# Four token groups instead of three in the input product of a hybrid decoder layer

## The chip, the cores and the metric

The kernel runs on one core of one Trainium2 chip, written in Bass with a tile framework that orders the instructions of each engine by priorities and sets the semaphores. The metric is the device time of one execution in microseconds. The profiler's record of one execution stands beside it, with start and duration of each instruction on TensorE (PE, with its weight loads as PEld), VectorE (DVE), ScalarE (ACT), GpSimd (POOL) and the DMA queues of SyncE (SP) and ACT.

## The reference

One layer of a decoder trunk on 1040 tokens (16 meta tokens ahead of 1024), width 1024, all float32. `h` is the layer-normed input. Cut to what matters:

```python
z = h @ w_in + b_in                       # 1024 -> 3840 columns
q, k, v, c_in, gates = split(z, [512, 640, 768, 1792])
a = swa_sink_attention(q, k, v, ...)      # window 128, 8 heads, 2 kv heads, sinks, T5 bias
y_attn = a @ w_attn_proj
c = c_val * sigmoid(c_gate)               # halves of c_in, 512 each
c = silu(layer_norm(causal_dwconv(c, 31 taps)))
y_conv = c @ w_conv_proj
mixed = sigmoid(g_attn) * y_attn + sigmoid(g_conv) * y_conv
h = layer_norm(alpha * h + mixed @ w_out)
u, g = split(causal_dwconv(h @ ffn_w_up, 3 taps), 2)
out = layer_norm(alpha * h + (gelu(g) * u) @ ffn_w_down)   # meta tokens dropped
```

## The kernel before

The layout is columns of `z` on the 128 partitions and tokens along the free dimension. A float32 product is made of float32r halves: weights and activations are each split into hi and lo, and every 128-row term of a product is three matmuls, hi·hi (L296), hi·lo (L300) and lo·hi (L301), in `product`. The sum over the 8 terms of K = 1024 is thus 24 matmuls into one PSUM tile, and each matmul loads its 128 × 128 weights anew.

`z` has 30 tiles of 128 columns. Three of them (k, v and the first q tile) belong to the lead-in (0 to 55 us), which also norms and transposes the input; its products are written out by hand in three token groups `HG` of 272, 384 and 384. The other 27 go through `z_tile`: for each token group, `z_group` takes a PSUM tile `ps_z` (three buffers), calls `product`, and hands the result to an evacuation. Their order is: convolution chunk 1 and 0 (two tiles each, gate and value), q tiles 1 to 3, gate tile 0, then gate tiles 1 to 15 and convolution chunks 2 and 3. Convolution tiles use the groups `HG`; q and gate tiles use `TG`, the same groups with the first 14 tokens (`U0`) left out, so 258, 384 and 384 columns.

The activations are in two arenas of 8320 columns, `RHO` (terms 0 to 3) and `RHC` (terms 4 to 7). `h0(k, hl, a, b)` gives the place of term k, half hl, tokens a to b. Before the change, each group has a region of its own: group 0 in slots of 272, groups 1 and 2 in slots of 384 from columns 272 and 3344 on (one slot of group 0 stays at 0, the others lie from 6144 on).

The evacuations: `q_evac` scales on ACT into a staging buffer (`stage`, in the arena `FA`), splits into `qsh` (ACT) and `qsl` (DVE), two buffers each, and stores both to `qd` in DRAM, the hi half on ACT's queue and the lo half on SP's. `gate_evac` (ACT, L672) takes a tanh into a staging buffer and stores it to `sgd` on ACT's queue. Convolution tiles stage the sigmoid of one tile (ACT) and multiply it into the other (DVE, L656); 31 taps of each chunk then run on DVE (L665), 1280 ns for each of the 120 later taps.

Attention is by blocks of 128 queries: `load_q` reads the queries back from `qd` into `qt`, the band scores are matmuls at L829 and L830, and the two queries ahead of the first block have small score matmuls (L749, L750). Priorities set the order: the band of attention stands ahead of the z tiles, so its matmuls are woven between those of the gate tiles. One edge is written by hand: the L749 matmuls are put behind a product term of gate tile 0, called `ahead`; `chunks_done` lists the first matmul of each product term, and before the change it takes the entry 2·8 + 1 after the tile's first. The edge orders instructions, and no semaphore is waited on for it.

After the z tiles come the branch projection (`ps_p`, L296 to L301 through the same `product`, with the groups `PG` of 258, 256, 256 and 256 tokens and the operand slots of `place`), the out product (`ps_w`), and the feed-forward's up (L1499) and down (L1637) products.

Of the kernel before, what the change touches and what calls it, by code (L numbers as in the profile page):

```python
# [31 lines left out]
KC = D // P  # L32
# [3 lines left out]
U0 = 14  # L36
# [14 lines left out]


HG = [(0, 272), (272, 656), (656, 1040)]
UG = [(0, 258), (258, 642), (642, 1026)]

PG = [(0, 258), (258, 514), (514, 770), (770, 1026)]
# [43 lines left out]
def tile_hybrid_layer(  # L100
# [9 lines left out]
    def load(o, i):  # L110
        return nc.sync.dma_start(out=o, in_=i)
# [5 lines left out]
    def f32(ap):  # L117
        return ap.bitcast(F)
# [6 lines left out]
    @contextmanager  # L125
    def rank(p):

        saved = tc.cur_priority
        tc.cur_priority = p
        yield  # L130
        tc.cur_priority = saved
# [9 lines left out]
    FA = arena.tile([P, 6144], F, name="FA")  # L141
    RHC = arena.tile([P, 8320], R, name="RHC")
    RHO = arena.tile([P, 8320], R, name="RHO")
# [62 lines left out]
    def bcol(m):  # L206
        return colA[:, m:m + 1]
# [43 lines left out]


    def h0(k, hl, a, b):
        g = next(g for g, x in enumerate(HG) if a < x[1])
        x, y = HG[g]
        i, n = (k % 4) * 2 + hl, y - x
        o = i * n + ((6144 if i else 0), 272, 3344)[g]
        return (RHO if k < 4 else RHC)[:, o + a - x:o + b - x]


    tc.cur_priority = RK_QKV
# [13 lines left out]
    def weights(shape, fill):  # L275
        fills[0] += 1
        n = fills[0]
        own = n == 3
        raw = sp.tile(shape, F, name="wr3") if own else wraw(shape)
        with rank({1: 13, 2: 18, 3: 17, 4: 23}.get(n, RK_SPLIT)):  # L280
            last_fill.append(fill(raw))
        hi, lo = (sp.tile(shape, R, name=t + "3") if own else wsp_p.tile(shape, R, name=t, tag=t)
                  for t in ("whi", "wlo"))
        if n <= 3:
            return hi, lo, raw
        with rank(RK_SPLIT):
            last_split.append(split(raw, hi, lo, True))
        return hi, lo

    chunks_done = []  # L290
# [13 lines left out]
    def z_group(wt, g, a, b, evac):  # L304
        hi, lo = wt
        ps = pat.tile([P, 512], F, name="ps_z", tag="mm", bufs=3)
        product(ps[:, :b - a], [(hi[:, k], lo[:, k], h0(k, 0, a, b), h0(k, 1, a, b)) for k in range(KC)])
        with rank(RK_EVAC):
            evac(g, a, b, ps[:, :b - a])

    def z_tile(fill, groups, evac, wt=None):
        wt = wt or weights([P, KC, P], fill)
        for g, (a, b) in enumerate(groups):
            z_group(wt, g, a, b, evac)

    def in_cols(m):
        return lambda raw: load(raw, w_z[m])

    TG = [(a + U0 if i == 0 else a, b) for i, (a, b) in enumerate(HG)]

    st_next = [0]

    def stage(n, lo=4104, cnt=5):
        i = st_next[0] % cnt
        st_next[0] += 1
        return FA[:, lo + i * 400:lo + i * 400 + n]

    tc.cur_priority = RK_QKV + 1000

# [15 lines left out]
    def q_evac(r):  # L345
        def evac(g, a, b, ps):
            t = stage(b - a)
            nc.scalar.activation(t, ps, AF.Identity, bias=qb[:, r:r + 1], scale=HD ** -0.5)
            h, l = (qsp.tile([P, 400], R, name=n, tag=n)[:, :b - a] for n in ("qsh", "qsl"))
            nc.scalar.copy(h, t)  # L350
            nc.vector.tensor_tensor(l, t, f32(h), OP.subtract)
            for hl, (put, x) in enumerate(((store, f32(h)), (load, f32(l)))):
                c = 0
                if g == 0:
                    c = P + 2
                    put(qd[:, (hl * 4 + r) * c:(hl * 4 + r + 1) * c], x[:, :c])
                n = (b - a - c) // P
                if n == 0:
                    continue
                i = (a - U0 + c) // P  # L360
                put(dram(qd, q_at(i) + (hl * 4 + r) * P, [[8 * U, P], [8 * P, n], [1, P]]),
                    x[:, c:].rearrange("p (n q) -> p n q", q=P))
        return evac
# [87 lines left out]
    def turns(g, *ks):  # L451
        n = len(GT[g])
        c = HG[g][1] - HG[g][0]
        at = {}
# [9 lines left out]
    def scaled(g, *ks):  # L464
        a, b = HG[g]
        for k in ks:
            tm = FA[:, 1044 + 272 * k:][:, :272] if g == 0 else sp.tile([P, 384], F, name="tm", tag="tm", bufs=5)
            ac(nc.scalar.activation(tm, turned[g, k], AF.Identity, bias=b0col(k), scale=g0col(k)))
            tms[g, k] = tm

    def parts(g, *ks, hi_act=()):
        a, b = HG[g]
        for k in ks:
            tm = tms[g, k]
            if k in hi_act:
                ac(nc.scalar.copy(h0(k, 0, a, b), tm))
            else:
                dv(V.tensor_copy(h0(k, 0, a, b), tm))
            dv(V.tensor_tensor(h0(k, 1, a, b), tm, f32(h0(k, 0, a, b)), OP.subtract))
# [131 lines left out]
    wt_c1 = [weights([P, KC, P], in_cols(m)) for m in (11, 7)]  # L611
# [30 lines left out]
    def conv_chunk(c):  # L642
        sig = {}

        def g_evac(g, a, b, ps):
            sig[g] = stage(b - a)

            nc.scalar.activation(sig[g], ps, AF.Tanh, bias=bcol(10 + c), scale=0.5)
            nc.scalar.activation(sig[g], sig[g], AF.Identity, bias=half_, scale=0.5)

        z_tile(in_cols(10 + c), HG, g_evac, wt_c1[0] if c == 1 else None)
        cin = cp.tile([P, 16 + T], F, name="cin", tag="cin")
        nc.vector.memset(cin[:, 0:16], 0.0)

        def v_evac2(g, a, b, ps):
            nc.vector.scalar_tensor_tensor(cin[:, 16 + a:16 + b], ps, bcol(6 + c), sig[g], OP.add, OP.mult)  # L656

        z_tile(in_cols(6 + c), HG, v_evac2, wt_c1[1] if c == 1 else None)
        with rank(RK_CONV + c * 100):
            for j in range(TAPS):  # L660
                wc = cdw[:, j * CH + c:j * CH + c + 1]
                if j == 0:
                    nc.vector.tensor_scalar(acc[c], cin[:, j:j + U], wc, cdwb(c), OP.mult, OP.add)
                else:
                    nc.vector.scalar_tensor_tensor(acc[c], cin[:, j:j + U], wc, acc[c], OP.mult, OP.add)  # L665

    def gate_tile(i):
        b2, m = divmod(i, KC)

        def gate_evac(g, a, b, ps):  # L670
            t = stage(b - a)
            nc.scalar.activation(t, ps, AF.Tanh, bias=bcol(14 + i), scale=0.5)  # L672
            store(sgd[b2, m, :, a - U0:b - U0], t)

        z_tile(in_cols(14 + i), TG, gate_evac)

# [31 lines left out]
    for q4 in range(2):  # L708
        ps = pat.tile([P, 512], F, name="ps_v4", tag="t", bufs=2)
        for i in range(4):  # L710
            c = NMETA + (q4 * 4 + i) * P
            nc.tensor.transpose(ps[:, i * P:(i + 1) * P], vT[:, c:c + P], ident)
        src = ps[:, :].rearrange("p (n g d) -> p n g d", g=2, d=HD)
        for g in range(NKV):
            hi, lo = (V[:, q4 * 4:q4 * 4 + 4, g, i] for i in range(2))
# [6 lines left out]
    for r in range(1, 4):  # L722
        z_tile(in_cols(r), TG, q_evac(r))

# [11 lines left out]
    tc.cur_priority = RK_Z - 500  # L736
    first_chunk = len(chunks_done)
    gate_tile(0)
    ahead = chunks_done[first_chunk + 2 * KC + 1]

    tc.cur_priority = RK_ATT

# [3 lines left out]
    for h in range(NH):  # L746
        g, r = divmod(h, 4)
        o = ps[:2, h * 16:(h + 1) * 16]
# [144 lines left out]
    with rank(RK_EVAC):  # L893
        nc.scalar.copy(c_hi[:, :U], csum)
        pinned.append(nc.vector.tensor_tensor(c_lo, csum, f32(c_hi[:, :U]), OP.subtract))
        for g, (a, b) in enumerate(UG):
            means[g] = pat.tile([P, 512], F, name="ps_m", tag="st"[g % 2], bufs=2)
# [40 lines left out]
    def cln_centre(g):  # L938
        a, b = UG[g]
        for c in range(CH):  # L940
            pin(dve.tensor_tensor(acc[c][:, a:b], acc[c][:, a:b], means[g][:, :b - a], OP.subtract))

    def cln_var(g):
        a, b = UG[g]
        n = b - a
        s_ = temp(n)
        nc.scalar.activation(s_, acc[0][:, a:b], AF.Square)
        for c in range(1, CH):
            q_ = temp(n)
            nc.scalar.activation(q_, acc[c][:, a:b], AF.Square)  # L950
            pin(dve.tensor_tensor(s_, s_, q_, OP.add))

        hi, lo = (conv(1, hl, a, b) for hl in range(2))
        pin(dve.tensor_copy(hi, s_))
        pin(dve.tensor_tensor(lo, s_, f32(hi), OP.subtract))
        sums[g] = pat.tile([P, 512], F, name="ps_m", tag="s", bufs=2)
        mean_mms(sums[g][:, :n], ones_r, hi, lo)

    def cln_rstd(g):
        n = UG[g][1] - UG[g][0]  # L960
        pv_, r_, t_ = sums[g][:, :n], temp(n), temp(n)
# [7 lines left out]
    def cln_scale(g):  # L969
        a, b = UG[g]  # L970
        for c in range(CH):
# [4 lines left out]
    def cln_split(g):  # L976
        a, b = UG[g]
        for c in range(CH):
# [101 lines left out]
    for m in range(KC):  # L1080
        hi, lo = weights([P, KC, P], lambda raw: load(raw, w_ab[m]))
# [299 lines left out]
    ahead = []  # L1381
# [4 lines left out]
    for i in (3, -1, 7, 2, 6, 0, 4, 1, 5):  # L1386
# [4 lines left out]
        ahead = [(i, *rows)]  # L1391
# [83 lines left out]
    for c in range(FC):  # L1475
        V4, X, Z, Y = (pup.tile([P, 1024], F, name=n, tag=n) for n in ("pw", "px", "pz", "py"))
        passes = ((1,), (0,)) if c == 0 else ((0, 1),)
        for subs in passes:
            last = subs == passes[-1]
            w_next = iter(range(7))  # L1480
            a, b = SUB[subs[0]][0], SUB[subs[-1]][1]
            i = max(a, 2)
# [308 lines left out]
```

## Time and profile before

| | |
|---|---|
| time, median of 3 runs | 1255.82 us (1255.19 to 1255.90) |
| the profiled execution's own time | 1255.65 us |
| its span | 1253.9 us |
| granted TensorE clock, mean | 0.999 |
| lead-in | 0 to 55 us |
| z tiles before the first gate tile | 55 to 136.5 us |
| z tiles with attention between them | 136.5 to 345 us |
| the last z tiles | 345 to about 415 us |
| branch projection, out product | to about 608 us |
| up product, down product and tail | to about 1036 us and 1254 us |

How to read it: the page gives busy time, its share of the span and the number of instructions of each engine; the chain is the work that ended last, followed back from the end; a wait row names the engine, the waiting tile and line, what released it, then the total in us, the count, and the longest. A timeline row gives start, duration, engine, line, operation, output and input tile, and size. A matmul's listed duration overlaps its neighbours', so rates come from starts. The stage borders above are where the first instructions of a stage start on PE, rounded.

### The profile page before, as it was taken

The page shows a single profiled execution, that of the slowest core. Times are in us where ns is not written, and L with a number is a line of the kernel's source. Part 1 is how long each engine was busy: PE and PEld are TensorE (multiplying, and loading weights), DVE is VectorE, ACT ScalarE, POOL GpSimd, SP SyncE. Part 2 cuts the span into 40 slices and gives each one's busy share as a digit, 9 for nine tenths or more (in the row PEclk, how much of TensorE's full clock was granted, in tenths as well). Part 3 has the DMA queues.
Part 4 walks back from the last instruction along what each step waited for, and adds up shares of the span by engine and source line. Part 5 has one row for each costly group of instructions (what it writes and reads, how often), then busy time and mean ns, then how long its engine had stood idle before and what let it go on. Part 6 is the DMA issues. An engine that isn't in the chain of part 4 may idle for free.

```text
span 1253.9 us, 21702 instructions
## 1 busy us (share of the span) xinstructions
PE 1241.6 (99%) x8546; PEld 1174.7 (94%) x8546; DVE 1081.1 (86%) x1876; ACT 586.7 (47%) x1056; POOL 12.3 (1%) x11
## 2 busy tenths in 40 slices
PE   9999999999999999999999999999999999999997
PEld 8999999999999999788899999999999998888886
DVE  7899989999978786648899999999999986996697
ACT  7522345645465233235565555554455553545330
POOL 0000000000000010000000000000000000000000
PEclk9999999999999999999999999999999999999999
DMA  7293733332255565222145565553464569988722
GB/s 280 71 312 103 183 107 95 109 93 87 68 147 142 182 173 139 77 75 101 68 135 187 192 210 189 186 215 120 167 218 167 204 207 318 387 317 315 251 85 84
DMA packets 96152, 212.10 MB, mean 169 GB/s; under 512 B 10787, under 2 KB 35939, under 8 KB 95922
## 3 DMA queue, kind: packets, MB, share of 16 engines
q1 hardware_dynamic: 84282, 199.64, 48.1%
q10 hardware_dynamic: 11768, 11.08, 2.7%
q8 instruction: 67, 1.10, 0.4%
q14 instruction: 35, 0.29, 0.1%
HBM read 150.29 MB, written 62.70 MB: 170 GB/s over the span
## 4 chain that ended last, share of the span: by engine, by line
PE 95%; DVE 3%; DMA 1%; issue 1%; ACT 0%; SPq 0%; DVEq 0%
PE px L1499 15%; PE py L1499 10%; PE ps_x L1637 9%; PE ps_z L1637 7%; PE ps_z L300 7%; PE ps_z L301 7%; PE ps_z L296 7%; PE pw L1499 5%; PE pz L1499 5%; PE ps_p L301 2%; PE ps_p L296 2%; PE ps_p L300 2%; PE ps_w L301 2%; PE ps_w L296 2%; PE ps_w L300 2%; PE ps_z L512 2%
## 5 line engine op out<-in xcount | busy, mean ns | idle before, releaser
L665 DVE SCALAR_TENSOR_TENSOR FA<-cin,cols,FA 128x1026 f32<-128x1026 f32 x120 | 152.5, 1280 | 0.3
L296 PE MATMUL ps_z<-RHO,whi 128*128 128x384 f32 (+2 forms) x324 | 104.2, 322 | 0.0
L300 PE MATMUL ps_z<-RHC,whi 128*128 128x384 f32 (+2 forms) x324 | 104.1, 321 | 0.0
L300 PE MATMUL ps_z<-RHO,whi 128*128 128x384 f32 (+2 forms) x324 | 104.0, 321 | 0.0
L301 PE MATMUL ps_z<-RHC,wlo 128*128 128x384 f32 (+2 forms) x324 | 103.8, 320 | 0.0
L296 PE MATMUL ps_z<-RHC,whi 128*128 128x384 f32 (+2 forms) x324 | 103.7, 320 | 0.0
L301 PE MATMUL ps_z<-RHO,wlo 128*128 128x384 f32 (+2 forms) x324 | 103.7, 320 | 0.0
L267 ACT CAST whi<-wr 128x1024 fp32r<-128x1024 f32 x37 | 39.0, 1053 | 69.1 <-PE ps_z L300 52.2
L1317 ACT CAST RHO<-wr 128x512 fp32r<-128x512 f32 x94 | 56.9, 621 | 24.2 <-DVE wr L1335 13.6
L1318 DVE TENSOR_TENSOR RHO<-wr,RHO 128x512 fp32r<-128x512 f32 x94 | 63.8, 690 | 4.5 <-ACT RHO L1317 4.2
L296 PEld LDWEIGHTS ps_z<-RHO,whi 128*128 128x128 f32 x324 | 61.0, 188 | 0.6 <-issue 0.3
L296 PEld LDWEIGHTS ps_z<-RHC,whi 128*128 128x128 f32 x324 | 61.1, 188 | 0.2
L301 PEld LDWEIGHTS ps_z<-RHO,wlo 128*128 128x128 f32 x324 | 61.0, 188 | 0.2
L301 PEld LDWEIGHTS ps_z<-RHC,wlo 128*128 128x128 f32 x324 | 60.9, 188 | 0.2
L1335 DVE TENSOR_TENSOR wr<-wr 128x512 f32<-128x512 f32 x88 | 61.0, 693 | 0.2
L300 PEld LDWEIGHTS ps_z<-RHO,whi 128*128 128x128 f32 x324 | 61.0, 188 | 0.1
L300 PEld LDWEIGHTS ps_z<-RHC,whi 128*128 128x128 f32 x324 | 60.9, 188 | 0.1
L672 ACT ACTIVATE FA<-ps_z,cols 128x384 f32<-128x384 f32 (+1 forms) x48 | 26.1, 543 | 50.3 <-PE ps_z L301 49.3
L1511 ACT COPY FA<-px 128x514 f32<-128x514 f32 (+2 forms) x23 | 13.2, 572 | 73.3 <-PE px L1499 73.3
L270 DVE TENSOR_TENSOR wlo<-wr,whi 128x1024 fp32r<-128x1024 f32 x35 | 42.6, 1218 | 4.8 <-ACT whi L267 4.1
L1318 DVE TENSOR_TENSOR ws<-wr,ws 128x512 fp32r<-128x512 f32 x60 | 40.9, 690 | 5.5 <-ACT ws L1317 5.3
L1424 ACT ACTIVATE FA<-OB,cols 128x512 f32<-128x512 f32 x44 | 36.0, 817 | 13.6 <-DVE OB L1507 13.6
(466 smaller groups left out, 3520.7 us busy)
## 6 DMA issues: line engine op xcount, KB each, us to landing
wr<-in_w_up_dram SPq DMA_DIRECT2D x44, 512.0 KB, 3.8
wr<-in_w_z_dram SPq DMA_DIRECT2D x30, 512.0 KB, 4.3
fd<-FA SPq DMA_DIRECT2D x44, 256.0 KB, 2.0
OB<-in_w_down_dram SPq DMA_DIRECT2D x19, 512.0 KB, 4.8
qt<-qd SPq DMA_DIRECT2D x28, 256.0 KB, 4.1
sgd<-FA ACTq DMA_DIRECT2D x32, 192.0 KB, 3.1
td<-OB SPq DMA_DIRECT2D x12, 512.0 KB
sums<-fd SPq DMA_DIRECT2D x12, 512.0 KB
```

Of the source, the lines that this page charges most:

```text
L267: ins = nc.scalar.copy(hi, raw)
L270: return (nc.vector if quick else nc.gpsimd).tensor_tensor(lo, raw, f32(hi), OP.subtract)
L296: ins = nc.tensor.matmul(ps, ah, bh, start=i == 0, stop=False)
L300: nc.tensor.matmul(ps, ah, bl, start=False, stop=False)
L301: last = nc.tensor.matmul(ps, al, bh, start=False, stop=i == n - 1)
L665: nc.vector.scalar_tensor_tensor(acc[c], cin[:, j:j + U], wc, acc[c], OP.mult, OP.add)
L1317: nc.scalar.copy(hi, src)
L1318: ins = nc.vector.tensor_tensor(lo, src, f32(hi), OP.subtract)
L1335: ins = nc.vector.tensor_tensor(*x)
L1424: nc.scalar.activation(t, cc[:, 2:HW], AF.Identity, bias=ffw(3, o), scale=ffw(2, o))
L1499: ins = nc.tensor.matmul(o, x[:, ks], bmat(sub, q, hl, k), start=first and k + j == 0, stop=k == 3 and j == 2, skip_group_check=not first)
L1637: nc.tensor.matmul(banks[i], l[:, ts], r[:, ws], start=first and a and x + k == 0, stop=z and x == len(ops) - 1 and k == 2, skip_group_che ...
```

## The change

The 27 tiles of `z_tile` use four groups, `ZG`: 272, 256, 256 and 256 tokens (258 in the first, for q and gate tiles, by `TG`). A tile has 96 matmuls and weight loads for 72, and four evacuations for three. The lead-in keeps `HG`.

`h0` has a new layout. Group 0's slots are as before but for which of them lie from 6144 on (those above index 2), and the other 768 tokens of a term and half lie in one slot of 768 columns, at 816 + i · 768. `stage` has two rings in `FA` from column 4136 on: seven buffers of 286 columns for groups up to 272, five of 400 for wider ones (those of the lead-in); before, it was one ring of five from 4104 on. `ahead` is the entry 8 + 18 after the tile's first, a term of the last group, for 2·8 + 1 before.

```diff
+ZG = [(0, 272), (272, 528), (528, 784), (784, 1040)]
...
     def h0(k, hl, a, b):
-        g = next(g for g, x in enumerate(HG) if a < x[1])
-        x, y = HG[g]
-        i, n = (k % 4) * 2 + hl, y - x
-        o = i * n + ((6144 if i else 0), 272, 3344)[g]
-        return (RHO if k < 4 else RHC)[:, o + a - x:o + b - x]
+        i = (k % 4) * 2 + hl
+        if a < 272:
+            o = i * 272 + (6144 if i > 2 else 0)
+        else:
+            o = 816 + i * 768 - 272
+        return (RHO if k < 4 else RHC)[:, o + a:o + b]
...
-    TG = [(a + U0 if i == 0 else a, b) for i, (a, b) in enumerate(HG)]
-
-    st_next = [0]
-
-    def stage(n, lo=4104, cnt=5):
-        i = st_next[0] % cnt
-        st_next[0] += 1
-        return FA[:, lo + i * 400:lo + i * 400 + n]
+    TG = [(a + U0 if i == 0 else a, b) for i, (a, b) in enumerate(ZG)]
+
+    st_next = [0, 0]
+
+    def stage(n):
+        big = n > 272
+        cnt, size = ((7, 286), (5, 400))[big]
+        o = 4136 + st_next[big] % cnt * size
+        st_next[big] += 1
+        return FA[:, o:o + n]
...
-        z_tile(in_cols(10 + c), HG, g_evac, wt_c1[0] if c == 1 else None)
+        z_tile(in_cols(10 + c), ZG, g_evac, wt_c1[0] if c == 1 else None)
...
-        z_tile(in_cols(6 + c), HG, v_evac2, wt_c1[1] if c == 1 else None)
+        z_tile(in_cols(6 + c), ZG, v_evac2, wt_c1[1] if c == 1 else None)
...
-    ahead = chunks_done[first_chunk + 2 * KC + 1]
+    ahead = chunks_done[first_chunk + KC + 18]
```

## The prediction

> **What bounds the kernel.** I read the page's busy shares first, then the chain that ended last, the waits of the five engines, and the busy time by stage.
>
> ```profile
> span 1253.9 us, 21702 instructions
> PE 1241.6 (99%) x8546; PEld 1174.7 (94%) x8546; DVE 1081.1 (86%) x1876; ACT 586.7 (47%) x1056; POOL 12.3 (1%) x11
> PE 95%; DVE 3%; DMA 1%; issue 1%; ACT 0%; SPq 0%; DVEq 0%
> 55.00:136.50 81.50, 81.50 (x520) 80.44 (x520) 77.77 (x95) 25.27 (x43) 0.00 (x0) 1.00 0.65 195
> 136.50:345.00 208.50, 207.61 (x1383) 202.58 (x1382) 199.42 (x405) 100.78 (x260) 0.00 (x0) 1.00 0.37 104
> 345.00:415.00 70.00, 70.00 (x448) 69.71 (x447) 56.60 (x118) 38.94 (x61) 0.00 (x0) 1.00 0.57 157
> PE ps_s L829 <- DMA qt<-qd: 0.9, 1, 0.9
> ```
>
> TensorE (PE) is busy for 99% of the span and carries 95% of the chain. The three window rows (length, then busy time and count of PE, weight loads, DVE, ACT and POOL, granted clock, DMA share, GB/s) cover the stage that the change edits: seven z tiles before the first gate tile, the z tiles between which attention is woven, and the last six. PE is full in the first and third, and in the second its missing 0.89 us is the one wait in the last row. The clock is at its full value. So this stage ends when PE has issued its matmuls, and the change is worth what it does to the distance between two matmuls, plus that wait. Everything that only ACT, DVE or a queue does is beside it, until PE waits for it.
>
> **The z product, per matmul.** A pipelined matmul's listed duration overlaps its neighbour's, so I use starts: the start of a group less the start of the next, over its 24 matmuls (8 terms of 3) or a multiple.
>
> ```profile
> 396.50 0.34 PE L296 MATMUL ps_z<-RHO,whi 128*128 128x384 f32 x1
> 404.82 0.28 PE L296 MATMUL ps_z<-RHO,whi 128*128 128x258 f32 x1
> 407.72 0.34 PE L296 MATMUL ps_z<-RHO,whi 128*128 128x384 f32 x1
> 418.93 0.28 PE L296 MATMUL ps_p<-OA,whi 128*128 128x256 f32 x1
> 427.41 0.28 PE L296 MATMUL ps_p<-OA,whi 128*128 128x258 f32 x1
> 430.31 0.29 PE L296 MATMUL ps_p<-OA,whi 128*128 128x256 f32 x1
> 438.49 0.28 PE L296 MATMUL ps_p<-OA,whi 128*128 128x258 f32 x1
> 607.92 1.41 PE px L1499 x12
> 660.95 2.72 PE py L1499 x24
> 1066.38 29.92 PE ps_x L1637 x132
> ```
>
> From 396.50 to 404.82 run the two 384-column groups of a tile: 8.32 us over 48, 173.3 ns each. The 258-column group after them takes 2.90 us (120.8 ns), and this group keeps its size. No z group is 256 wide, but the branch projection that follows is exactly the new form: the same helper, 258 + 3 × 256, whose operands already lie in the slots that the new z layout copies (group 0 at i × 272, then 768 columns for each term and half from 816 on). It shows two rates. From 418.93 to 427.41 its 72 matmuls take 8.48 us, 117.8 ns each; in the next tile, from 430.31 to 438.49, 8.18 us, 113.6 ns. The chain's rows of the up product have the same pair: 1.41 us / 12 = 117.5 and 2.72 / 24 = 113.3. The rate holds through a tile and then changes, so it looks like a state that a tile falls into; I can't see from the trace what sets it. 512 columns cost 29.92 / 132 = 226.7 ns, twice 113.3.
>
> Per tile, two groups of 384 cost 8.32 us. Three of 256 cost 8.18 (good) or 8.48 (bad): 0.14 less or 0.16 more. Over the 27 z tiles that is −3.8 us or +4.3 us, and it breaks even where 47% of the tiles are bad. This is the whole question of the change, and the trace brackets it on both sides of zero. The tiles shown of the projection, the nearest code, go half and half; the up product is mostly at the good rate and falls to 117.5 after a break in its stream. In the middle of the z stage, matmuls of attention break the stream again and again. I take 40% bad: 27 × (−0.14 + 0.4 × 0.30) = −0.5 us.
>
> The rows also allow another reading. The z tile's own two forms lie on a line: (173.3 − 120.8) / 126 = 0.417 ns a column and 13.3 ns for the matmul, and 512 columns lie on it too (226.8). By that line a 256-column matmul costs 120.0, and it is a rival below. Against it stand 113.3 and 117.8, measured on 256 columns.
>
> The Trainium skill, "TensorE: Matmul & The Clock Gate", section "Back-to-back issue gap", has such a line: N / 2.4 ns plus a fixed 2.5 ns for an isolated matmul. By it alone the 27 × 24 = 648 added matmuls would be +1.6 us (an estimate from that page). This trace shows its slope, 0.417, but not its constant.
>
> **Weight loads.** The change also adds 648 weight loads. Transposes of 128 columns, whose operand is a new weight each time, bound how fast a load can follow a load.
>
> ```profile
> 304.79 1.03 PE L853 MATMUL ps_t<-cols,s 128*128 128x128 f32 x8
> ```
>
> Eight in 1.03 us, the last one's drain included, are at most 129 ns each. That bound lies above 113.3, so it alone would not exclude that loads set the pace; but the projection and the up product load a weight for every matmul and run at 113.3, so I put zero on it beyond the two rates.
>
> **The wait for the first queries, and `ahead`.**
>
> ```profile
> 136.53 0.28 PE L296 MATMUL ps_z<-RHO,whi 128*128 128x258 f32 x1
> 139.43 0.34 PE L296 MATMUL ps_z<-RHO,whi 128*128 128x384 f32 x1
> 140.47 0.34 PE L296 MATMUL ps_z<-RHO,whi 128*128 128x384 f32 x1
> 141.70 0.33 PE L829 MATMUL ps_s<-kx,qt 128*128 128x144 f32 x1 [0.89 <-DMA qt<-qd]
> 145.72 0.34 PE L296 MATMUL ps_z<-RHO,whi 128*128 128x384 f32 x1
> 145.90 0.17 PE L749 MATMUL ps_s<-kx,qt 128*2 128x16 f32 x1
> 118.77 5.46 DMA qd<-qsl
> 132.84 2.88 DMA qd<-qsl
> 136.30 5.36 DMA qt<-qd
> ```
>
> `ahead` names the product term behind which the eight small score matmuls of L749 come; they start at 145.90, right behind the term's matmul at 145.72. It says nothing of the band scores of L829, and those are what waits. In terms of the first gate tile the edit moves L749 from the second term of group 2 to the third of group 3. In PE time: before, 2.90 + 4.16 + 3 × 0.173 = 7.6 us after the tile's start; after, 2.90 + 2 × 2.73 + 6 × 0.114 = 9.0. So L749 and the softmax of that small block come about 1.4 us later; behind it queue only its own DVE and ACT steps and the L750 matmuls, and z matmuls fill PE meanwhile. Cost 0; were it not covered, 1.4.
>
> The band scores at 141.70 waited because the queries were read back (5.36 us) only after their last piece was stored. PE lost 1.23 us from 140.47 to 141.70, of which 0.17 is a matmul: 1.06 us. With 256-column groups, the order of PE's instructions is laid out anew and the L829 matmuls may fall a little later or earlier against the load. I take half: −0.5 us. Bounds: −1.06 (gone) and, if the queries come late, the third rival.
>
> **The store chain of q1 to q3.** Each q tile now has 4 groups with 5 stores of each half (hi on ACT's queue, lo on SP's) where 3 groups had 4: +3 on each queue, and the 16 gate tiles put 16 more stores on ACT's. The lo halves go through two buffers, freed by the landing of the store.
>
> ```profile
>   DMA qd<-qsl: 2.0, 2
> DMA to landing us min/median/max: 2.8/4.3/6.5
> 124.32 0.56 DVE L351 TENSOR_TENSOR qsl<-FA,qsh 128x384 fp32r<-128x384 f32 x1 [1.65 <-DMA qd<-qsl]
> 132.38 0.42 DVE L351 TENSOR_TENSOR qsl<-FA,qsh 128x258 fp32r<-128x258 f32 x1
> ```
>
> DVE waited for such a landing twice, 2.0 us in all. A group now comes every 2.7 us instead of 4.16, and one buffer is held for the DVE step plus 2.8 to 5.5 us, so two buffers pass one each 1.6 to 3.0 us: near the edge. The added issues lie beside PE; I book 0 and keep the rest for the rival.
>
> **Evacuations.**
>
> ```profile
> L672 ACT ACTIVATE FA<-ps_z,cols 128x384 f32<-128x384 f32 x32 | 18.5, 577 | 36.8 <-PE ps_z L301 36.3 <-PE ps_m L888 0.5
> L672 ACT ACTIVATE FA<-ps_z,cols 128x258 f32<-128x258 f32 x16 | 7.6, 475 | 13.5 <-PE ps_z L301 12.9 <-ACT FA L672 0.5
> L656 DVE SCALAR_TENSOR_TENSOR cin<-ps_z,cols,FA 128x384 f32<-128x384 f32 x8 | 4.9, 610 | 1.7 <-PE ps_z L301 1.7
> L1099 DVE SCALAR_TENSOR_TENSOR OB<-OB,ps_p 128x256 f32<-128x256 f32 x21 | 8.8, 420 | 7.0 <-PE ps_p L301 6.9
> ```
>
> Gate tiles: 48 × 0.475 = 22.8 us of ACT for 18.5. Convolution tiles: 12 × 0.420 = 5.0 us of DVE for 4.9; the q split, 9 × 0.42 for 6 × 0.56, adds 0.4. PE is what ACT waits for in these rows (36.3 us), and with three PSUM buffers an evacuation has two groups, 5.4 us, before PE needs its buffer. Cost 0. The cover is DVE's: 199.42 of 208.50 in the middle stage, so 0.6 us more still fits; if not, up to 0.6. The staging buffers, moved off the columns that the key rows use and more in number, remove a possible hold on ACT only: 0. The lead-in products keep 384 columns but read at another distance from the weights: 0, within ±0.6 (3 tiles × 48 matmuls × the 4.2 ns between the two rates).
>
> **Sum.** −0.5 − 0.5 = −1.0 us on the profiled 1255.65 gives 1254.65; the median of the runs is 0.17 higher: 1254.8.
>
> **Rivals.** *Good state throughout.* The new slots put every term at one distance from the weights and the long runs before 136.5 and after 345 are unbroken; then −3.8 and −1.06 give 1251.0. Against: the projection has the same slots and shows both rates. *Slower: the 117.8 ns state is the rule,* set anew at each 258-column group and by each attention matmul. +4.3 − 0.0 gives 1260.1; it decides from 47% bad tiles up, and the projection's tile at 418.93 speaks for it. *Slower: the q stores fall behind,* the queries land about 3 us later (one more landing of 2.9) and the wait at L829 grows from 0.9 to 3.9: 1255.82 − 0.5 + 3 = 1258.3; for it the two waits of DVE, against it that 258-column store landed in 2.88. *Slower by much: a fixed price for every matmul,* the line through 258, 384 and 512 columns: 24 × (3 × 120.0 − 2 × 173.3) ns × 27 = +8.7, 1264.5; the z tile's own forms speak for it, every 256-column row against it. The section of the Trainium skill named above has the same shape with a smaller constant. *The edit of `ahead` does nothing:* it doesn't order L829, the wait stays: 1255.3, inside the forecast's own spread.
>
> **How the numbers follow.** 0.2% is 2.5 us, about what a measurement of this kernel tells from no change. Mixed states 0.39 (own range 1252.3 to 1257.5): 0.11 faster, 0.26 same, 0.02 slower. Good 0.27: 0.24 faster, 0.03 same. Bad 0.17: 0.14 slower, 0.03 same. Late queries 0.08: 0.05 slower, 0.03 same. Fixed price 0.09: 0.08 slower, 0.01 same. Sum: faster 0.35, same 0.36, slower 0.29. The range goes from 1250.4 (good, and 0.6 off the lead-in) to 1260.2 (bad throughout); it leaves out nearly all of the fixed price, and the edges.
>
> **What would show it.** Right: 256-column z groups between 2.72 and 2.83 us apart with both rates present; PE busy near 100% in all z windows; the L829 wait under 1 us; more ACT time at L672 and no wait of PE for it. Wrong: a rate outside 113 to 118 ns for 256 columns (weight loads or the layout cost something unseen); PE waiting for `qt` for 2 us or more; a wait of PE on a `ps_z` buffer; or a change in the projection or the lead-in, where I booked nothing.

## The result, and the profile after

The changed kernel takes 1262.11 us (median of 6, 1260.20 to 1266.09) beside 1255.86 us, a ratio of 1.0054 (95% interval 1.0044 to 1.0064). Measured again, in the first experiment, it was 1261.17 us against 1255.90, 1.0038 (1.0026 to 1.0051). It is slower: its three quickest runs (1260.20 to 1260.38) lie 4.5 us above the median of the kernel before, and the other three take 3.5 to 5.8 us more than these; the kernel before spreads over 1 us.

The page of one of its quickest executions (1260.31 us) and its waits of PE:

```profile
span 1258.5 us, 23087 instructions
PE 1242.1 (99%) x9194; PEld 1176.1 (93%) x9194; DVE 1081.3 (86%) x1883; ACT 595.6 (47%) x1088; POOL 12.3 (1%) x11
PE 91%; DMA 3%; DVE 3%; ACT 2%; issue 1%; SPq 0%; ACTq 0%; DVEq 0%
```

```profile
PE ps_h L467 <- DVE xn L431: 1.9, 1, 1.9
PE ps_z L299 <- DVE cin L661: 1.7, 1, 1.7
PE ps_z L299 <- ACT FA L677: 1.5, 2, 0.8
PE ps_s L834 <- DMA qt<-qd: 0.5, 1, 0.5
```

PE has 648 more matmuls and its busy time is 0.5 us longer; DVE is as busy as before, ACT 8.9 us busier (586.7 us before). What is new are waits of PE for a `ps_z` buffer, 3.2 us in three places, and the chain now holds 2% of ACT and more DMA. (Lines are those of the changed kernel: L299 to L304 is the product, L661 the convolution's value evacuation, L677 that of the gates.)

Where the 4.66 us between the two profiled executions lie can be read from three starts: the first z matmul, the first projection matmul, and the end.

```profile
56.49 0.39 PE L296 MATMUL ps_z<-RHO,whi 128*128 128x272 f32 x1
416.04 0.28 PE L296 MATMUL ps_p<-OA,whi 128*128 128x258 f32 x1
```

```profile
57.16 0.39 PE L299 MATMUL ps_z<-RHO,whi 128*128 128x272 f32 x1
420.57 0.28 PE L299 MATMUL ps_p<-OA,whi 128*128 128x258 f32 x1
```

The first fence is the kernel before, the second the changed one. The lead-in ends 0.67 us later; the z stage takes 363.41 us for 359.55, 3.86 more; behind it 0.13 is added. The z stage's 3.86 is +3.2 of new waits, −0.4 from the wait for the first queries (0.9 to 0.5), and about 1.0 that remains for the matmuls. With the waits taken out, the distances behind all z matmuls of the stage sum to 309.58 us for 307.71, 1.9 more, and those behind the matmuls of attention to 50.10 for 50.94, 0.8 less.

How the first wait comes about (DVE's rows and PE's):

```profile
75.02 1.21 DVE L273 TENSOR_TENSOR wlo<-wr,whi 128x1024 fp32r<-128x1024 f32 x1
76.16 2.34 DVE L450 TENSOR_TENSOR OB<-OB,gb 128x1024 f32<-128x1024 f32 x2
78.43 1.26 DVE L661 SCALAR_TENSOR_TENSOR cin<-ps_z,cols,FA 128x272 f32<-128x272 f32 x3
78.96 0.38 PE L299 MATMUL ps_z<-RHO,whi 128*128 128x256 f32 x1 [1.71 <-DVE cin L661]
```

By the profile the first group of convolution chunk 1's value tile is complete at 71.60, but DVE works off the residual's scalings and a weight split, in its order, and takes the result at 78.43. PE has three `ps_z` buffers. It has filled the other two with 256-column groups by 77.25 and waits. Before, the same DVE work stood in the same place, and the evacuation of the group, complete at 71.08, came as late, 6.7 us behind:

```profile
77.76 1.00 DVE L656 SCALAR_TENSOR_TENSOR cin<-ps_z,cols,FA 128x272 f32<-128x272 f32 x2
```

There PE needed the buffer only at 79.25, after two groups of 4.16 us. The other two waits are of the same kind on ACT (rows of ACT and of the matmuls behind, changed kernel):

```profile
377.76 1.28 ACT L677 ACT_TABLE_LOAD   x1
379.05 0.47 ACT L677 ACTIVATE FA<-ps_z,cols 128x256 f32<-128x256 f32 x1
379.58 0.39 PE L299 MATMUL ps_z<-RHO,whi 128*128 128x256 f32 x1 [0.75 <-ACT FA L677]
385.95 1.28 ACT L979 ACT_TABLE_LOAD   x1
387.25 1.90 ACT L979 ACTIVATE FA<-FA,cols 128x384 f32<-128x384 f32 x3
389.06 0.45 ACT L677 ACTIVATE FA<-ps_z,cols 128x256 f32<-128x256 f32 x1
389.57 0.39 PE L299 MATMUL ps_z<-RHO,whi 128*128 128x256 f32 x1 [0.74 <-ACT FA L677]
```

The first of these evacuations stands behind a load of its own function table (1.28 us), the second behind a load of another table and three activations of the convolution's norm. Their groups were complete at 373.13 and 383.02, so ACT came 5.9 and 6.0 us later. Each narrow group takes 2.7 us of PE where a wide one took 4.2, so the time that a late evacuation may take fell from 8.3 us to 5.4, and these three were later than that. (A fourth, started at 382.33 for a group complete at 376.00, was 6.3 us late; PE, held back by the wait at 379.58, came to its buffer later and did not wait.) Before, the two latest gate evacuations are these:

```profile
378.65 0.46 ACT L672 ACTIVATE FA<-ps_z,cols 128x258 f32<-128x258 f32 x1
387.23 0.57 ACT L672 ACTIVATE FA<-ps_z,cols 128x384 f32<-128x384 f32 x1
```

Their groups were complete at 373.87 and 382.55, so they start 4.8 and 4.7 us later and are done after 5.2, well inside 8.3.

The distances of the matmuls, at the end of the z stage, where nothing stands between them (first matmul of each group):

```profile
401.05 0.29 PE L299 MATMUL ps_z<-RHO,whi 128*128 128x256 f32 x1
403.78 0.28 PE L299 MATMUL ps_z<-RHO,whi 128*128 128x256 f32 x1
406.50 0.28 PE L299 MATMUL ps_z<-RHO,whi 128*128 128x256 f32 x1
409.22 0.28 PE L299 MATMUL ps_z<-RHO,whi 128*128 128x258 f32 x1
412.09 0.28 PE L299 MATMUL ps_z<-RHO,whi 128*128 128x256 f32 x1
414.92 0.28 PE L299 MATMUL ps_z<-RHO,whi 128*128 128x256 f32 x1
417.75 0.28 PE L299 MATMUL ps_z<-RHO,whi 128*128 128x256 f32 x1
```

One tile runs at 2.72 us a group (113.3 ns a matmul), the next at 2.83 (117.8). Over all 1,835 intervals between two 256-column z matmuls of this trace, 862 are near 113, 916 near 118 and 57 longer. Their mean, without those that hold a wait, is 117.5 ns; 1,196 intervals of 384 columns before have a mean of 175.4. 648 × (3 × 117.5 − 2 × 175.4) ns is +1.1 us for the product; the sums above, which hold the first groups and the run-up behind each wait too, give 1.9, and attention's 0.8 less hides part of it.

### The profile page after: what moved, and what is told of

The parts are those of the page before. It is cut to its first block, busy times and chain, and to the rows that moved or that the text cites. A ratio compares the mean times of both kernels' runs of the same rounds, so it can differ in the third digit from the quotient of the medians.

```text
span 1258.5 us, 23087 instructions
## 1 busy us (share of the span) xinstructions
PE 1242.1 (99%) x9194; PEld 1176.1 (93%) x9194; DVE 1081.3 (86%) x1883; ACT 595.6 (47%) x1088; POOL 12.3 (1%) x11
## 4 chain that ended last, share of the span: by engine, by line
PE 91%; DMA 3%; DVE 3%; ACT 2%; issue 1%; SPq 0%; ACTq 0%; DVEq 0%
PE px L1504 14%; PE py L1504 9%; PE ps_x L1642 9%; PE ps_z L1642 7%; PE ps_z L299 6%; PE ps_z L303 6%; PE ps_z L304 6%; PE pz L1504 5%; PE pw L1504 5%; PE ps_p L299 2%; PE ps_p L304 2%; PE ps_p L303 2%; PE ps_w L304 2%; PE ps_w L299 2%; PE ps_w L303 2%; PE ps_z L517 2%
## 5 line engine op out<-in xcount | busy, mean ns | idle before, releaser
L299 PE MATMUL ps_z<-RHO,whi 128*128 128x256 f32 (+2 forms) x432 | 122.5, 284 | 3.2 <-DVE cin L661 1.7
L303 PE MATMUL ps_z<-RHO,whi 128*128 128x256 f32 (+2 forms) x432 | 122.0, 282 | 0.0
L303 PE MATMUL ps_z<-RHC,whi 128*128 128x256 f32 (+2 forms) x432 | 122.0, 282 | 0.0
L304 PE MATMUL ps_z<-RHO,wlo 128*128 128x256 f32 (+2 forms) x432 | 121.6, 281 | 0.0
L299 PE MATMUL ps_z<-RHC,whi 128*128 128x256 f32 (+2 forms) x432 | 121.5, 281 | 0.0
L304 PE MATMUL ps_z<-RHC,wlo 128*128 128x256 f32 (+2 forms) x432 | 121.4, 281 | 0.0
L299 PEld LDWEIGHTS ps_z<-RHO,whi 128*128 128x128 f32 x432 | 81.3, 188 | 4.2 <-DVE cin L661 1.9
L304 PEld LDWEIGHTS ps_z<-RHC,wlo 128*128 128x128 f32 x432 | 81.5, 189 | 0.3
L304 PEld LDWEIGHTS ps_z<-RHO,wlo 128*128 128x128 f32 x432 | 81.6, 189 | 0.1
L303 PEld LDWEIGHTS ps_z<-RHC,whi 128*128 128x128 f32 x432 | 81.3, 188 | 0.3
L299 PEld LDWEIGHTS ps_z<-RHC,whi 128*128 128x128 f32 x432 | 81.3, 188 | 0.3
L303 PEld LDWEIGHTS ps_z<-RHO,whi 128*128 128x128 f32 x432 | 81.4, 188 | 0.0
L677 ACT ACTIVATE FA<-ps_z,cols 128x258 f32<-128x258 f32 (+1 forms) x64 | 30.2, 472 | 62.3 <-PE ps_z L304 55.2
L1322 ACT CAST ws<-wr 128x512 fp32r<-128x512 f32 x60 | 36.2, 619 | 13.2 <-DVE wr L1340 7.3
```

The source lines that it names most:

```text
L299: ins = nc.tensor.matmul(ps, ah, bh, start=i == 0, stop=False)
L303: nc.tensor.matmul(ps, ah, bl, start=False, stop=False)
L304: last = nc.tensor.matmul(ps, al, bh, start=False, stop=i == n - 1)
L1322: nc.scalar.copy(hi, src)
```

## Experiments

Theory W, for waits: the loss is in the three waits for `ps_z` (3.2 us idle; I put 3.7 on them with what PE takes to run up behind each, an estimate). Its rival R: the 256-column matmuls' slower rate. The first four kernels ran on one chip.

**The changed kernel again.**

> The changed kernel once more, beside the others on one chip. Theory W (waits for PSUM): its quick runs are 4.5 us over the kernel before, of which 3.7 us are three waits of PE for a ps_z buffer (one behind DVE's cin evacuation near 77 us, two behind ACT's gate evacuation near 378 and 388 us), 0.7 us a later start of the first z tile, the matmul rate is worth under 0.5 us. Theory R (rate): the 256-column matmuls in the slow state are the loss, and the waits cover each other. Both expect 1260.2 again, and W expects the three waits in the same places. The runs 3 to 6 us above that had a granted clock of 0.995 to 0.997 for 0.998; if they come again, the profile may show where the clock was lost.

1261.17 us (1260.13 to 1261.55). The same three waits, 1.7 and 1.6 us, in the same places; the wait for the first queries is 1.2 us this time.

**The edge alone put back.**

```diff
-    ahead = chunks_done[first_chunk + KC + 18]
+    ahead = chunks_done[first_chunk + 2 * KC + 1]
```

> The changed kernel with the edge of the eight small score matmuls back at the entry 17 after the gate tile's first. W and R: within 0.5 us of the changed kernel, since the edge binds only those matmuls; the wait at the first band scores stays between 0.4 and 1.1 us. Rival: the edge sets the order of all of attention, then the time moves by 1 us or more.

1262.56 us (1261.29 to 1266.17), ratio 1.0053 (1.0038 to 1.0068): 1.4 us more than the changed kernel of the same call, with overlapping intervals. The quickest run is 1.2 us over the changed kernel's quickest. I had given it 0.5 at most. That the edge itself costs anything is not shown: the z stage takes 366.15 us here and 364.32 in the first experiment, and the difference is what a halved clock explains (1.7 us, below). The trace shows how it came:

```profile
379.00:380.00 1.00, 0.39 (x4) 0.19 (x2) 0.00 (x0) 1.00 (x2) 0.00 (x0) 1.00 0.00 0
380.00:381.00 1.00, 0.14 (x1) 0.14 (x2) 0.53 (x1) 1.00 (x3) 0.00 (x0) 1.00 0.00 0
382.00:383.00 1.00, 0.98 (x6) 0.98 (x7) 1.00 (x2) 0.54 (x2) 0.00 (x0) 0.83 0.41 57
384.00:385.00 1.00, 1.00 (x6) 1.00 (x6) 0.93 (x3) 0.99 (x2) 0.00 (x0) 0.50 0.86 330
387.00:388.00 1.00, 1.00 (x11) 1.00 (x11) 0.96 (x4) 1.00 (x3) 0.00 (x0) 1.00 0.02 3
```

These are windows of 1 us: length, busy time and count of PE, of its weight loads, of DVE, ACT and POOL, granted clock, DMA share, GB/s. Near 380 PE stands idle for 1.47 us behind ACT, and 0.31 us more a little later:

```profile
380.86 0.39 PE L299 MATMUL ps_z<-RHO,whi 128*128 128x256 f32 x1 [1.47 <-ACT FA L677]
382.02 0.44 PE L892 MATMUL ps_m<-OC,ones_r 128*128 128x384 f32 x1 [0.31 <-DVE OC L959]
```

From 382.65 on (0.83 in that window) the granted clock is 0.50, for 3.41 us, and PE starts 6 matmuls a microsecond for 11. The waits thus cost themselves and, here, half of 3.41 us on top. It is not the rule: six waits of PE of 1.70 to 1.86 us behind the lead-in, in five of the traces, this one's of 1.71 us near 78 among them, were not followed by it. The mean clock of a run is a sign of it: all runs of the changed kernel up to 1261.6 us have 0.998 or 0.999, those at 1263.83, 1265.06 and 1266.09 have 0.997, 0.995 and 0.995. As 0.001 of this span is 1.3 us, the clock accounts for about 1 to 4 of the 3.5 to 5.8 us that these runs take longer; none of them has a trace, and the rest of their spread is open.

The Trainium skill, "TensorE: Matmul & The Clock Gate", section "What's actually happening", has the clock halved after an idle window of about 3.4 us, windows that run freely of 3413 ns. The length of the halved stretch agrees (3.41 us, and 6.83, about 2 × 3.41, in a kernel below). What went ahead of it does not: here it was 1.47 us of idle PE and 0.31 more a microsecond later.

**Only the layout.** Three groups, with the new slots and rings and the old edge (the edge's line as above).

```diff
-ZG = [(0, 272), (272, 528), (528, 784), (784, 1040)]
+ZG = HG
```

> Three groups of 272, 384 and 384 with the new slots, the new staging rings and the old edge: only where things lie is changed. W: 1255.9 within 1 us, no waits for ps_z, the 384-column matmul at 173.3 ns. Rival (the new distance costs): 384-column matmuls off 173.3 ns or the lead-in later by 0.7 us, so up to 1258. If the first z tile starts 0.7 us later here too, the lead-in loss belongs to the layout.

1257.09 us, ratio 1.0009 (1.0000 to 1.0018). (In this kernel the two staging rings share columns, so a convolution tile's first staged group is overwritten before it is used and the output is not the layer's; the work is the same.) No wait for `ps_z`. But the layout is not free: the 384-column matmul has a second state too, which it never had in a clean group of the kernel before.

```profile
400.84 0.34 PE L299 MATMUL ps_z<-RHC,whi 128*128 128x384 f32 x1
405.08 0.34 PE L299 MATMUL ps_z<-RHC,whi 128*128 128x384 f32 x1
```

The same term of two groups, 4.24 us and 24 matmuls apart: 176.7 ns, for 173.3. 620 of 1,196 intervals are between 176 and 180 ns, against 92 before. The lead-in is not slower for the layout: from DVE's first `xn` to the first z matmul it takes 46.6 to 46.7 us in all fourteen traces. That `xn` starts between 9.78 and 10.62, at 9.79 before and 10.53 in the changed kernel, where DVE had waited 0.86 us for the first `x` to land. No edit touches that load.

**Two groups in one PSUM tile.** The second and third group of a tile are put into one 512-column buffer.

```diff
-        ps = pat.tile([P, 512], F, name="ps_z", tag="mm", bufs=3)
+        if g != 2 or len(groups) < 4:
+            bank[0] = pat.tile([P, 512], F, name="ps_z", tag="mm", bufs=3)
+        ps = bank[0][:, 256:] if g == 2 and len(groups) == 4 else bank[0]
```

> The changed kernel, but the second and third group of a tile share one PSUM tile of 512 columns, so a buffer comes round after a whole tile (11 us) as before the change, not after three groups (8.3 us). W: the three waits go, 1260.2 - 3.7 = 1256.5, within 1 us. R: 1260 still, since the rate is what costs.

1263.77 us, ratio 1.0057 (1.0043 to 1.0071): a miss. The order of PE's instructions came out otherwise (in some tiles one matmul of the first group, then the whole second group), the waits stayed, and the queries came late:

```profile
PE ps_s L838 <- DMA qt<-qd: 3.3, 1, 3.3
PE ps_z L299 <- ACT FA L681: 2.4, 2, 1.9
PE ps_z L299 <- DVE cin L665: 1.7, 1, 1.7
```

From 146.51 on, within the 3.3 us (they end at 147.12), the clock is at half for 6.83 us. This kernel doesn't tell W from R, as the waits were not taken away. It shows what late queries cost, and that 1,275 of its 1,813 intervals of 256 columns are at the good rate, which suggests that the states depend on the order (tried below).

**The distance of the slots from the weights.** The slots of the second to fourth group lie 64 bytes from the weights (modulo 256) in the kernel before, 192 in the changed one, worked out from the programs: weights and arenas take multiples of 256 bytes, and the slots start 272 × 4 = 1088 and 816 × 4 = 3264 bytes into an arena. (Only the slots move in these runs. Whether the distance from the weights counts, or the place itself, they can't tell apart; distance is the name used here.) How many of group 0's slots lie ahead sets it:

```diff
-            o = i * 272 + (6144 if i > 2 else 0)
+            o = i * 272 + (6144 if i > 0 else 0)
...
-            o = 816 + i * 768 - 272
+            o = 272 + i * 768 - 272
```

> The changed kernel with one slot of group 0 ahead of the 768-column slots for three, so that these lie 64 bytes (modulo 256) from the weights as in the kernel before, and not 192. Theory D (distance): layout alone had put the 384-column matmul from 173.3 to 176.7 ns on most tiles; at the old distance every clean 256-column group runs at 113.4 ns and the time falls by about 4 us against the changed kernel, to 1256 to 1257, with the ps_z waits still there (3.7 us). Rival (lock by history): the state is set by what ran before, good and bad stay about half and half, 1260 to 1261.

1263.65 us, ratio 1.0067 (1.0054 to 1.0080), 2.5 us over the changed kernel. Distance matters, in the other direction: at 64 bytes 384 columns run at their good rate (the kernel before) and 256 at their bad one (1,652 intervals bad, 123 good).

```profile
405.60 0.28 PE L299 MATMUL ps_z<-RHC,whi 128*128 128x256 f32 x1
408.43 0.28 PE L299 MATMUL ps_z<-RHC,whi 128*128 128x256 f32 x1
411.25 0.28 PE L299 MATMUL ps_z<-RHC,whi 128*128 128x256 f32 x1
```

**The waits taken away.** Convolution chunk 1 and gate tiles 11 to 13 go back to 272 (258), 384 and 384, with the wide staging ring; the other 22 tiles keep four groups.

```diff
...
+        wide[0] = c == 1
+        G = HG if wide[0] else ZG
...
+        wide[0] = i in (11, 12, 13)
+        z_tile(in_cols(14 + i), [(U0, 272)] + HG[1:] if wide[0] else TG, gate_evac)
```

> The changed kernel with its own slots (distance 192), but convolution chunk 1 and gate tiles 11, 12 and 13 in groups of 272 (258), 384 and 384. W: the three waits go, 3.7 us less than the changed kernel, 1256.5 to 1258, and no run has the clock at half outside the end. R: 1260.

1256.93 us (11 runs, 1255.83 to 1260.16), ratio 1.0010 (1.0001 to 1.0018): 4.2 us under the changed kernel of the first experiment. All waits of PE of 0.3 us or more in its trace:

```profile
PE ps_w L543 <- DVE ones_r L221: 1.1, 1, 1.1
PE pw L1511 <- ACT FA L1312: 1.0, 1, 1.0
PE ps_h L469 <- DVE xn L433: 0.5, 1, 0.5
PE ps_z L516 <- ACT FA L475: 0.3, 1, 0.3
PE px L1511 <- ACT OB L1523: 0.3, 1, 0.3
```

The wait for `ps_z` behind a z evacuation is gone, and the one for the first queries too. Its z stage takes 359.59 us, what it takes in the kernel before. W holds: with five tiles of 27 widened the loss is gone, while 56% of the 256-column intervals are still bad (820 of 1,467). The distances behind its z matmuls sum to 309.68 us, for 309.58 in the changed kernel: the widening took 3.7 us of waits out of the z stage (0.5 of them for the queries) and nothing off the rate. R's part is there but small: 2.0 us over the kernel before, nearly balanced by attention's matmuls (1.0 less) and the missing wait for the queries (0.9). One run of 11 had a clock of 0.997 (1260.16 us), where I had expected none; the kernel before had one such of 15 (1258.71).

**The same at 64 bytes** from the weights:

> As the kernel with the old distance, and in addition convolution chunk 1 and gate tiles 11, 12 and 13, where PE waited for ps_z, go back to groups of 272 (258), 384 and 384. W with D: no wait for ps_z, all groups at their good rates: 1252.5 to 1253.5, quicker than the kernel before. W without D: 1256.5 to 1257.5. Neither: 1260.

1259.79 us, ratio 1.0031 (1.0019 to 1.0043). No wait of more than 0.2 us for `ps_z` in the z tiles; 2.9 us over the last kernel, of which (120.4 − 118.6) ns × 1,466 = 2.6 is the rate of the 256-column matmuls. By my bounds this is neither, but I had not priced the rate at 64 bytes into them. Beside the kernel with the same slots and the waits (1263.65) it is 3.9 us less, nearly the step of 4.2 at 192 bytes: W again. D, all 256-column groups at the good rate at 64 bytes, is refuted.

**The reverse.** Three groups everywhere at 64 bytes with the old edge, four only in convolution chunk 1 and gate tiles 11 to 13.

> The reverse: three groups everywhere and the old distance, four groups only in convolution chunk 1 and gate tiles 11, 12 and 13. W: the waits come back with five narrow tiles: 1255.9 + 3.5, so 1258.5 to 1259.5, some runs 2 to 6 us above by a halved clock. R: within 0.7 us of the kernel before.

1258.23 us, ratio 1.0020 (1.0011 to 1.0029), 2.5 us over the kernel before from five tiles. One wait came back, the first: 1.4 us behind DVE's `cin`. The two on ACT did not. The five tiles' own rate (117.8 at this distance) adds 5 × 24 × (3 × 117.8 − 2 × 173.3) ns = 0.8 us. Against that the wait for the queries is 0.6 us shorter, and the distances behind the matmuls of attention are 1.3 us longer in sum (52.23 for 50.94). The waits are less than I had put on them, and no run was stretched by more than 1.7 us. So five narrow tiles bring back one wait of the three: whether an evacuation on ACT is late depends on how the tiles around it fall.

**Two other distances,** with the five wide tiles: all slots of group 0 behind the others, or two ahead.

> The kernel with the five wide tiles, all 768-column slots right from column 0 on: 0 bytes (modulo 256) from the weights, where 192 gave 118.6 ns a 256-column matmul over the whole stage (61% of the intervals bad) and 64 gave 120.6 (99% bad). If distance sets the share of the bad state, this run shows a third share: all good would be 1256.9 - 1488 x 5.2 ns = 1249 at the least and 1252 to 1253 by the clean groups; all bad 1259.8. If only history sets it, 1257 within 1 us.

> The same with two slots of group 0 ahead, 128 bytes (modulo 256) from the weights. Distance sets the share: somewhere between 1252 and 1260, off 1257 by over 1 us in one direction; the clean 256-column groups all at one rate. History: 1257 within 1 us, both rates. I have no reason to expect one sign.

1261.27 and 1261.26 us, ratios 1.0043 (1.0031 to 1.0056) and 1.0043 (1.0029 to 1.0057): both 4.3 us over the kernel with 192 bytes, and above the bound that I had given for 0 bytes. None waits for `ps_z` in a z tile. The rows are groups without anything between, at 0 bytes:

```profile
108.63 0.28 PE L299 MATMUL ps_z<-RHC,whi 128*128 128x256 f32 x1
111.51 0.28 PE L299 MATMUL ps_z<-RHC,whi 128*128 128x256 f32 x1
```

2.88 us, 120.0 ns. What a clean group showed at each distance, ns a matmul:

| bytes, modulo 256 | 256 columns | 384 columns |
|---|---|---|
| 0 | 120.0 | 173.3 to 174.9 |
| 64 | 117.8, a few tiles 113.3 | 173.3 |
| 128 | 118.5 to 120.1 | 176.1 |
| 192 | 113.3 or 117.8 | 173.3 or 176.7 |

History alone is excluded: apart from the tiles left wide, only the slots' place differs between these kernels.

**Interleaving the first group.** With the five wide tiles and 192 bytes, one or two matmuls of the first group go ahead of the whole second group, the rest behind it.

```diff
...
+            for g, k, j in steps[0][:1] + steps[1] + steps[0][1:]:
...
```

> The kernel with the five wide tiles at distance 192, and in every four-group tile one matmul of the first group, then the whole second group, then the other 23 of the first. In the kernel with paired PSUM tiles the order came out so by itself, and 73% of its 256-column intervals were in the good state. Theory H (at this distance the state is handed on from one matmul to the next, and the 258-column ones set it): nearly all 256-column groups good, 852 bad intervals x 4.4 ns = 3.7 us off 1256.9, so 1253.2 to 1254, quicker than the kernel before. Rival (the good share of the paired kernel came from its timing): 1257 within 1 us.

> The same with two matmuls of the first group ahead, so 22 behind. If it is an odd or even number of 258-column matmuls that flips the state, this one stays mixed or bad: 1257 to 1259. If any interleaving does it, as quick as with one.

1256.95 us, ratio 1.0015 (1.0006 to 1.0023), and 1258.49 us, ratio 1.0029 (1.0019 to 1.0039). In the stretches without attention the good share rose from 27% to 76% with one ahead and to 60% with two, so the order bears on the state, and an odd or even number alone doesn't decide. The 1253.2 to 1254 that I expected of it is missed: between the matmuls of attention the share stayed under half (47%, 44% and 42%), and a new wait for ACT's gate evacuation (0.7 us) took more than half of the 1.3 us won on 256-column matmuls (one ahead); the first z matmul also came 0.9 us later than in the kernel with the five wide tiles, with the first `x`. No kernel tried beats the kernel before.

## Why the prediction was wrong

- **What bounds the kernel**: right. PE, its matmul distances and its waits are all that counts; the other engines' added work is not in the sum.
- **The step that failed is "Evacuations"**, which put 0 on them because "an evacuation has two groups, 5.4 us, before PE needs its buffer". I compared those 5.4 us with the half microsecond that an evacuation takes, and not with when DVE and ACT come to it. In the rows above both have other work ahead of it, and the rows of the kernel before already held the answer: `cin` taken at 77.76 for a group complete at 71.08, 6.7 us. That is over 5.4. The average busy share (the cover was argued from DVE's 199.42 of 208.50 us in the middle stage, where no such wait came) was the wrong view; a better one is, for each evacuation, its start less the end of its group. Measured: 3.2 us of waits, about 4 us of time by the kernel with five wide tiles. A wait of PE on a `ps_z` buffer was named among the signs of being wrong.
- **How far that view would have gone.** It foretells the wait behind DVE, 1.7 of the 3.2 us. On ACT it left the matter open: in the kernel before, the two latest gate evacuations (at 378.65 and 387.23) are done 5.2 us after the end of their groups, just under 5.4. In the changed kernel, where ACT's other work lies differently among more and shorter evacuations, the two that PE waits for start after 5.9 and 6.0.
- **The sum.** The profiled execution was forecast at 1254.65 us and took 1260.31. The 5.7 us between are 3.2 of waits for `ps_z`, 1.5 of matmul distances (+1.0 in the z stage with attention's, for −0.5), 0.1 of the wait for the queries, 0.7 of the lead-in and 0.1 behind the z stage.
- **What the waits cost beyond themselves** was in no step: the halved clock, 1.7 us for each stretch of 3.41 us. By their mean clocks, half of the runs of the first measurement had such stretches. They put that median 1.9 us above the range; in the first experiment, where all clocks are 0.998 or 0.999, the median is still 1.0 us above, and the quickest runs, 1260.1 and 1260.2, lie at its upper end.
- **The z product**: the bracket of 113.6 and 117.8 held, and so did mixed states; the share was 52% bad, not 40%, and with the longer intervals around attention the term is +1.1 us, not −0.5. That the slots' place and the order bear on the state I could not see; "same slots, both rates" was right for 192 bytes, the one distance that shows both.
- **The fixed price per matmul** (120.0 ns), a rival, is what 0 bytes shows, but not the changed kernel.
- **The wait for the first queries**: 0.5 and 1.2 us in two executions for 0.9, so half of it gone was no gain that lasts. The late queries of the third rival came in the kernel with paired buffers (3.3 us), not in the changed one.
- **`ahead`**: put at 0; the edge put back cost 1.4 us in the median, with overlapping intervals, and in the profiled run a halved clock behind a wait for ACT (1.47 us at once) explains it. A cost of the edge itself is not shown, and whether the edge leads to that wait is open.
- **The lead-in**: no cost of the layout, as booked; it ends up to 0.9 us apart from run to run, by when the first `x` is normed, and 0.7 of the 4.66 us is such a difference.

The rival that ended slower in the forecast, the 117.8 ns state throughout, gave nearly the right time (1260.1) for the wrong reason, by luck: about half of the tiles were in that state, and the waits made up the rest. The narrow tiles at 64 bytes are nearest to what it looks like, another 2.5 us up with the waits.

## What to carry to other kernels

Before tiles are made narrower, take for each evacuation the time from the end of its group to its start, not its duration, and hold it against the buffers less one times the new group time: an engine with spare time on average is still late behind its queue. A delay just under that bound is no cover either: the change moves it. A wait of PE of 1.5 us was once followed by a halved clock that cost 1.7 us more, so a change that adds a few waits should be judged by the spread of its times as well. And a rate measured on one tile belongs to its width and the place of its operands: compare the same width at the same distance before pricing it.

## What was not expected of the hardware

- The distance between two matmuls depends on where the moving operand lies modulo 256 bytes (against the weights, or as such; only the operand was moved): 113.3 to 120.1 ns for 256 columns, 173.3 to 176.7 for 384. At 64 bytes 384 columns run at their best and 256 hardly ever do.
- At 192 bytes there are two states that last for whole tiles, and one matmul of the first group set ahead of the second raised the good share from 27% to 76% in the stretches without attention.
- The clock fell to half for 3.41 us behind 1.47 us of waiting and 0.31 more a microsecond later, but not behind six single waits of 1.70 to 1.86; what decides is not settled here.
